# One-hot operands of the PEER gate products, built token by token on VectorE

## The chip, the cores and the metric

The kernel runs on one core of one Trainium2 chip. The metric is the device time of one execution in microseconds. Before the change three runs took 1708.99, 1710.05 and 1712.87 us, median 1710.05 us. The profiled execution, from which all rows below come, took 1712.26 us.

## The reference, cut to what matters

The program is one layer of a diffusion backbone over 512 latent tokens of width 1024 (with 256 context tokens): a mixing part (windowed attention and a gated delta rule), then PEER, a retrieval of single-neuron experts. The change lies in PEER alone:

```
q = (xt @ w_query)                        # 8 heads x 2 halves of 128
s = q . sub_keys                          # 128 keys per half
s_top, i_top = top_k(s, 16)               # per half
best, pos = top_k(all 16 x 16 sums, 16)   # per head
expert = i1 * 128 + i2                    # 128 (head, k) pairs per token, 16384 experts
gate = softmax(best)
act = gelu(u_tab[expert] . xt)
y = sum over the 128 pairs of gate * act * v_tab[expert]
```

Each token thus has 128 triples (i1, i2, gate).

## The kernel before, in words

The 512 tokens lie in four tiles (slots 0 to 3) of 128. For slot 3 the kernel gathers the rows of `peer_u` and `peer_v` that its tokens want (GpSimd indirect DMAs, line 2224, with VectorE sums, lines 2234 and 2256). For slots 0 to 2 (384 tokens) it computes all 16384 experts densely, in 128 blocks e of 128 experts:

- **U product** (`t_usplit`, `t_u`, `t_act`): a block of `peer_u` is loaded, split into two 16-bit parts (ScalarE line 2056, VectorE line 2058, one operation of 1024 elements each), multiplied with the tokens (24 TensorE matmuls of 384 columns through `mm`, line 207) and passed through Gelu (ScalarE line 2091). The split has two slots, so it runs at most two blocks ahead of the matmuls. Results wait in SBUF for the V stage; the number of places for them is limited, and up to 20 more may be written to DRAM.
- **Gates** (`t_gates`, the functions of the diff): a dense 128 x 128 matrix of gates per token, as a product of one-hot matrices. For one token, with its 128 pairs on the partitions, the left operand is onehot(i1), the right one onehot(i2) times the gate; the gate is carried as a high and a low float16 part, so there are two right operands and two 128-column matmuls per token. TensorE transposes i1, i2 and gate of a slot so that the pairs come onto the partitions (line 1952); `pT` holds the transposed columns, one column per token. Then eight chunks of 16 tokens follow per slot, 24 chunks in all. In a chunk VectorE builds three operand blocks `oh[0..2]` of 16 tokens x 128 keys with four whole-chunk operations (lines 1980, 1982, 1984, 1986); TensorE does 32 matmuls into four PSUM banks; ScalarE copies them out (line 1998); a DMA writes the chunk to DRAM (`wd`, line 2003).
- **V product** (`t_wread`, `t_vload`, `t_vsplit`, `t_g`, `t_v`): from the event `ev_wall` on, when all gates have been written, gates are read back, multiplied with the U results (lines 2147, 2152, 2154), `peer_v` is split (lines 2131, 2133), and each block costs 18 matmuls of 512 columns.

The order of each engine's instructions is fixed when the program is built: a planner (`Driver`) simulates the engines with a cost for each step (`dv`, `ac`, `p16`, the table `X`) and hands out the steps by priority (a lower number first; U split 60.5, gates 70 to 72, U matmuls 80.7). On the chip each engine works through its list in that order and waits where a semaphore makes it wait. In `dv(n, p, x)` the planner takes 0.068 us, plus n x 1.042 ns divided by x, plus 0.062 us for each of p scalars per partition.

Of the kernel before, what the change touches and what calls it, by code (L numbers as in the profile page):

```python
# [17 lines left out]
F16 = mybir.dt.float16  # L18
# [3 lines left out]
AF = mybir.ActivationFunctionType  # L22
OP = mybir.AluOpType
# [43 lines left out]
class Driver:  # L67
# [26 lines left out]
    def _advance(self, t, val):  # L94
        while True:
# [20 lines left out]
            else:  # L116
                t.pend = s
                if s[0] == "PE" and t.ready == t.pe:
                    t.ready -= X['lPE']
                self.ready.append(t)  # L120
                return

    def run(self):
        while self.ready or self.blocked:
# [14 lines left out]
            starts = [max(t.ready, self.free[t.pend[0]]) for t in self.ready]  # L139
            m = min(starts) + X['win']  # L140
            i = min((k for k in range(len(starts)) if starts[k] <= m),
# [4 lines left out]
            self.free[e] = end  # L146
            end += X["l" + e]
            if len(t.pend) > 2:
# [7 lines left out]
def get(res, n=1):  # L156
    return ("get", res, n)


def put(res, *items):  # L160
    return ("put", res) + items


def p16(n, m=1):
    return ("PE", m * max(0.027, n / 2400.0 + 0.0025))


def p32(n, m=1):
    return ("PE", m * max(0.107 * X["f32"], n * 0.429 * X["f32"] / 512))


def ptr32(m):
    return ("PE", 0.109 * m)


def dv(n, p=0, x=1):
    return ("DVE", 0.068 + n * 1.042e-3 / x + 0.062 * p)


def ac(n, p=0, sb=0):  # L180
    return ("ACT", 0.051 + 0.042 * sb + n * 0.833e-3 + 0.093 * p)
# [6 lines left out]
def dm(nbytes):  # L188
    return ("DMA", nbytes / 360e3)


def later(step):
    return step + ("a",)


X = {'ch': 6.183, 'gt': 9.96, 'ka': 11.636, 'qa': 6.328, 'z': 10.883, 'ad2': 8.509, 'wo': 14.584, 'a1': 5.91, 'a2': 9.456, 'a0': 10.73, 'a3': 11.524, 'o1': 14.974, 'o2': 11.058, 'o0': 14.074, 'o3': 15.009, 'p00': 4.186, 'p01': 1.683, 'p10': 3.269, 'p11': 4.66, 'p20': 3.974, 'p21': 2.21, 'p30': 5.555, 'p31': 5.48, 'p40': 4.392, 'p41': 9.258, 'p50': 5.369, 'p51': 6.667, 'vg': 0.857, 'ga': 5.978, 'k': 5.749, 'v': 4.787, 'q': 5.8, 'cs': 6.278, 'ro': 10.195, 'vi': 3.54, 'hx': 5.748, 'lPE': 0.1405, 'lDVE': 0.1984, 'lACT': 0.18, 'lPOOL': 0.1344, 'lDMA': 2.0, 'win': 0.1972, 'f32': 2.175, 'pt': 60.784, 'ps': 61.1, 'pg': 70, 'pgc': 70, 'pul': 80.08, 'pus': 60.5, 'pu': 80.677, 'pvs': 75, 'pgg': 74.921, 'pv': 81.055, 'pga': 77, 'pgt': 78, 'pq': 60, 'psc': 60, 'pql': 18, 'pqs': 18, 'pac': 80, 'ptg': 75.5, 'psg': 75.6}


def layer(tc, io, dbg=None):
# [16 lines left out]
def _body(tc, nc, V, A, G, PE, io, dbg, drv, sync, mm, ap_, pp_, dp_):  # L216
# [337 lines left out]
    ev_ada2 = Ev()  # L554
    AD2 = X["ad2"]

# [215 lines left out]
    def evac(dst, b, n, ev, bank):  # L772
        yield ac(n)
        A.activation(dst, b[:, :n], AF.Copy, scale=1.0 / WS)
        yield put(bank, b)
        yield ("set", ev)

    def t_qkv(kind, h, ti):
# [9 lines left out]
        ev_raw = Ev()  # L788
        yield ("spawn", evac(raw[:, 2:514], b, T, ev_raw, bank), X[kind] + 0.1 * h)
        if not lat_only:  # L790
# [848 lines left out]
    for n, t in enumerate((1, 2, 0, 3)):  # L1639
        drv.add(t_out(t), X["o%d" % t])  # L1640

    _peer(nc, V, A, G, PE, io, dbg, drv, sync, mm, reg, bk, bc, Bump, gp4, at3, obk, h2hl, h2d, x1d, modrow, dp_,
          sm, cst, ident, TILE, ev_h2, ev_gdn, ev_attall, ev_odone, stats, bnhalf, moments, fetch)
    drv.run()
# [6 lines left out]
def _peer(nc, V, A, G, PE, io, dbg, drv, sync, mm, reg, bk, bc, Bump, gp4, at3, obk, h2hl, h2d, x1d, modrow, dp_,  # L1651
# [40 lines left out]
    grow = Res([reg(69 + 4 * i, [D]) for i in range(4)])  # L1692
    ust = Res([reg(17 + 4 * i, [KT, 128]) for i in range(3)])
    uhl = Res([(reg(29 + 4 * i, [KT, 128], F16), reg(31 + 4 * i, [KT, 128], F16)) for i in range(2)])
    ohs = Res([[reg(101 + 12 * i + 4 * j, [16, 64, 2], F16) for j in range(3)] for i in range(2)])
    wbs = Res([reg(125 + 8 * i, [128, 16]) for i in range(2)])
    pTs = Res([[reg(141 + 0.5 * (4 * i + j), [128, 2], F16) for j in range(4)] for i in range(2)])
    iota = reg(145, [64, 2], F16)
    vst = Res([reg(101 + 4 * i, [D]) for i in range(3)])
    vhl = Res([(reg(113 + 4 * i, [D], F16), reg(115 + 4 * i, [D], F16)) for i in range(2)])  # L1700
    wrs = Res([reg(121 + 12 * i, [NCH, 8, 16]) for i in range(2)])
# [2 lines left out]
    def actr(kb, n):  # L1704
        return [reg(kb + 1.5 * i, [ND]) for i in range(n)]
# [236 lines left out]
    def t_gates(s):  # L1942
        yield ev_pair[s]
        yield ev_qdone
        yield ev_iota
        k = pairs[s]
        ii = k["ii"]
        b = yield get(wvb)
        ps = bk(b, [3, 128])
        yield ptr32(3)  # L1950
        for n in range(3):
            PE.transpose(ps[:, n], ii[:, n].rearrange("p k h -> p (k h)"), ident)
        yield put(tks, k)
        pT = yield get(pTs)
        def twice(n):
            return bc(ps[:, n, :, None], 128, 2)
        for n in range(2):
            yield later(ac(256))
            A.activation(pT[n], twice(n), AF.Copy)
        yield ac(256)  # L1960
        A.activation(pT[2], twice(2), AF.Copy, scale=1024.0)
        yield dv(256)
        V.scalar_tensor_tensor(pT[3], twice(2), 1024.0, pT[2], op0=OP.mult, op1=OP.subtract)
        yield ("join",)
        yield put(wvb, b)
        left = [8]
        done = Ev()

        def chunk(n):
            tk = slice(n * 16, n * 16 + 16)  # L1970
            oh = yield get(ohs)

            def col(i):
                return bc(pT[i][:, tk, None], 16, 64, 2)
            keys = iota[:, None].to_broadcast([128, 16, 64, 2])

            def row(i, tok):
                return oh[i][:, tok].rearrange("p a b -> p (a b)")
            yield later(dv(2048, 0, 2))
            V.tensor_tensor(oh[0], col(0), keys, op=OP.is_equal)  # L1980
            yield dv(2048, 0, 2)
            V.tensor_tensor(oh[1], col(1), keys, op=OP.is_equal)  # L1982
            yield later(dv(2048, 0, 2))
            V.tensor_tensor(oh[2], oh[1], col(3), op=OP.mult)  # L1984
            yield later(dv(2048, 0, 2))
            V.tensor_tensor(oh[1], oh[1], col(2), op=OP.mult)  # L1986
            yield ("join",)
            wb = yield get(wbs)
            for q in range(4):
                b = yield get(wvb)  # L1990
                ps = bk(b, [4, 128])
                yield p16(128, 8)
                for j in range(4):
                    tok = q * 4 + j
                    mm(ps[:, j], row(0, tok), row(1, tok), j == 0, False)
                    mm(ps[:, j], row(0, tok), row(2, tok), False, j == 3)
                yield later(ac(512))
                A.activation(wb[:, :, q * 4:q * 4 + 4], ps.rearrange("p t i -> p i t"), AF.Copy, scale=GS / 1024.0)  # L1998
                yield put(wvb, b)
            yield put(ohs, oh)  # L2000
            yield ("join",)
            yield dm(128 * 8192)
            sync.dma_start(wd[:, :, s * 8 + n].rearrange("w p i t -> p w i t"), wb.rearrange("p (w i) t -> p w i t", i=8))
            yield put(wbs, wb)
            left[0] -= 1
            if left[0] == 0:
                yield ("set", done)
        for n in range(8):
            yield ("spawn", chunk(n), X["pgc"] + s)
        yield done  # L2010
        yield put(pTs, pT)
        yield ("set", ev_gated[s])
        w_left[0] -= 1
        if w_left[0] == 0:
            yield ("set", ev_wall)
# [4 lines left out]
    def t_iota():  # L2020
        yield ev_qdone
        yield ev_mem1
        yield dm(128 * 256)
        sync.dma_start(iota.rearrange("p a b -> p (a b)"), io["iota"])
        yield put(ohs, [reg(73 + 4 * j, [16, 64, 2], F16) for j in range(3)])
        yield ("set", ev_iota)
        for s in range(3):
            yield ev_pair[s]
        yield put(acts, *acts1)
        for s in range(3):  # L2030
            yield ev_gated[s]
        yield get(tks, 2)
        yield put(acts, *actr(85, 8))
        yield put(tks, tks_late[0])
        yield ev_pair[3]
        yield put(acts, *acts2)
# [284 lines left out]
    for s in range(4):  # L2321
        drv.add(t_slot(s), X['ps'] + 0.2 * s if s != GSLOT else X['psg'])
    drv.add(t_iota(), 60)
    for s in range(3):
        drv.add(t_gates(s), X['pg'] + s)
# [108 lines left out]
```

## Time and profile before

| | before |
|---|---|
| runs | 1708.99, 1710.05, 1712.87 us |
| profiled execution | 1712.26 us, span 1710.5 us |
| TensorE (PE) busy | 1609.8 us, 94% of the span |
| VectorE (DVE) busy | 1444.0 us, 84% |
| ScalarE (ACT) busy | 791.0 us, 46% |
| GpSimd (POOL) busy | 478.1 us, 28% |
| mean granted TensorE clock | 0.984 of full speed |

"Span" is the time from the first to the last recorded instruction of the profiled execution; the execution lasted 1.8 us longer than its span. Busy time is a union: where two instructions of one engine overlap, the overlap counts once. The duration of an instruction is therefore longer than what it costs its engine when another follows at once; that cost is the distance from start to start, and is read from the timeline.

### The profile page before, as it was taken

The page shows a single profiled execution, that of the slowest core. Times are in us where ns is not written, and L with a number is a line of the kernel's source. Part 1 is how long each engine was busy: PE and PEld are TensorE (multiplying, and loading weights), DVE is VectorE, ACT ScalarE, POOL GpSimd, SP SyncE. Part 2 cuts the span into 40 slices and gives each one's busy share as a digit, 9 for nine tenths or more (in the row PEclk, how much of TensorE's full clock was granted, in tenths as well). Part 3 has the DMA queues.
Part 4 walks back from the last instruction along what each step waited for, and adds up shares of the span by engine and source line. Part 5 has one row for each costly group of instructions (what it writes and reads, how often), then busy time and mean ns, then how long its engine had stood idle before and what let it go on. Part 6 is the DMA issues. An engine that isn't in the chain of part 4 may idle for free.

```text
span 1710.5 us, 29276 instructions
## 1 busy us (share of the span) xinstructions
PE 1609.8 (94%) x11075; PEld 978.2 (57%) x11075; DVE 1444.0 (84%) x2884; ACT 791.0 (46%) x1386; POOL 478.1 (28%) x351
## 2 busy tenths in 40 slices
PE   3999998988896999999999999999999999899997
PEld 1665557887655885677655555555555554444443
DVE  3678658988989999999988888888888888798887
ACT  2665658766533434566543333333333333244441
POOL 0200332323001000000014445445466556554300
PEclk9999999999998999999999999999999999999999
DMA  9335442211333303699969999999999999888762
GB/s 378 113 128 187 155 179 81 70 56 45 109 112 134 114 2 124 191 272 279 325 241 354 348 369 344 374 364 350 347 377 330 367 363 331 315 317 331 270 244 86
DMA packets 157727, 405.16 MB, mean 237 GB/s; under 512 B 12681, under 2 KB 71561, under 8 KB 152465
## 3 DMA queue, kind: packets, MB, share of 16 engines
q1 hardware_dynamic: 120720, 269.06, 45.1%
q0 software_dynamic: 36864, 134.23, 21.4%
q8 instruction: 86, 1.41, 0.3%
q14 instruction: 57, 0.46, 0.1%
HBM read 366.59 MB, written 36.65 MB: 236 GB/s over the span
## 4 chain that ended last, share of the span: by engine, by line
PE 39%; DVE 20%; DMA 10%; issue 5%; POOL 2%; ACT 1%; POOLq 0%; DVEq 0%; ACTq 0%; SPq 0%
PE bank L207 38%; DMA arena<-in_peer_v,arena 8%; DVE arena L2058 3%; POOL arena L2224 2%; DVE arena L1986 1%; DVE arena L1984 1%; DVE arena L1980 1%; DVE arena L1982 1%; DVE arena L2256 1%; DMA arena<-in_peer_u,arena 1%; DVE arena L1816 1%; DVE arena L1818 1%; DVE arena L1822 1%; DVE arena L1814 1%; DVE arena L1759 1%
## 5 line engine op out<-in xcount | busy, mean ns | idle before, releaser
L207 PE MATMUL bank<-arena 128*128 128x384 f16 (+9 forms) x10610 | 1566.5, 316 | 49.4 <-DVE arena L1105 6.8
L207 PEld LDWEIGHTS <-arena 128*128 128x128 f16 (+1 forms) x9528 | 826.9, 98 | 626.8 <-issue 46.1
L2224 POOL DMA_INDIRECT arena<-in_peer_u,arena x128 | 161.1, 1258 | 515.2 <-DMA arena<-in_peer_ut 339.0
L2224 POOL DMA_INDIRECT arena<-in_peer_v,arena x128 | 211.8, 1655 | 160.6 <-DVE arena L2256 140.4
L2056 ACT ACTIVATE arena<-arena 128x1024 f16<-128x1024 f32 x128 | 135.1, 1056 | 253.9 <-PE bank L207 184.5
L2131 ACT ACTIVATE arena<-arena 128x1024 f16<-128x1024 f32 x128 | 134.2, 1050 | 136.4 <-PE bank L207 101.0
L2256 DVE SCALAR_TENSOR_TENSOR arena<-arena 128x1024 f32<-128x1024 f32 x126 | 160.2, 1280 | 36.9 <-DMA arena<-in_peer_v,arena 36.7
L2133 DVE TENSOR_TENSOR arena<-arena 128x1024 f16<-128x1024 f32 x128 | 156.0, 1219 | 29.2 <-ACT arena L2131 29.0
L2058 DVE SCALAR_TENSOR_TENSOR arena<-arena 128x1024 f16<-128x1024 f32 x128 | 155.9, 1220 | 26.5 <-ACT arena L2056 26.3
L2234 DVE SCALAR_TENSOR_TENSOR arena<-arena 128x1024 bf16<-128x1024 f32 x128 | 156.3, 1221 | 23.6 <-DMA arena<-in_peer_u,arena 22.8
L2152 ACT ACTIVATE arena<-arena 128x384 f16<-128x384 f32 x128 | 66.4, 519 | 170.6 <-DVE arena L2147 170.4
L207 PEld LDWEIGHTS bank<-arena 128*128 128x128 f32 (+1 forms) x1082 | 114.5, 178 | 36.0 <-DMA arena<-in_w_ada 12.3
L2154 DVE TENSOR_TENSOR arena<-arena 128x384 f16<-128x384 f32 x128 | 70.6, 552 | 6.6 <-ACT arena L2152 6.6
L1063 POOL TENSOR_TENSOR arena<-arena 128x512 f32<-128x512 f32 x12 | 17.9, 1495 | 203.7 <-DVE arena L1060 203.7
L2147 DVE TENSOR_TENSOR arena<-arena 128x384 f32<-128x384 f32 x128 | 70.5, 551 | 1.5 <-DMA arena<-wd 1.5
L1998 ACT ACTIVATE arena<-bank 128x512 f32<-128x512 f32 x96 | 51.7, 598 | 24.9 <-PE bank L207 17.8
L1105 DVE TENSOR_TENSOR arena<-bank,arena 128x512 f16<-128x512 f32 x72 | 49.0, 685 | 15.9 <-PE bank L207 11.5
L2091 ACT ACTIVATE arena<-bank 128x384 f32<-128x384 f32 x128 | 60.7, 475 | 1.6 <-DVE arena L2154 1.2
L1113 ACT ACTIVATE arena<-bank 128x512 f16<-128x512 f32 x60 | 35.8, 597 | 22.4 <-PE bank L207 21.3
L810 DVE SCALAR_TENSOR_TENSOR arena<-arena 128x770 f32<-128x770 f32 (+1 forms) x48 | 44.1, 928 | 0.8
L1529 POOL TENSOR_TENSOR arena<-arena 128x1024 f32<-128x1024 f32 x4 | 9.4, 2348 | 116.5 <-DVE arena L1527 104.0
L1118 ACT ACTIVATE arena<-bank 128x512 f16<-128x512 f32 x60 | 35.5, 596 | 6.2 <-PE bank L207 4.5
(256 smaller groups left out, 1275.0 us busy)
## 6 DMA issues: line engine op xcount, KB each, us to landing
arena<-in_peer_ut SPq DMA_DIRECT2D x128, 512.0 KB, 5.8
arena<-in_peer_v SPq DMA_DIRECT2D x128, 512.0 KB, 6.4
arena<-in_w_ada SPq DMA_DIRECT2D x24, 1024.0 KB, 8.7
wd<-arena SPq DMA_DIRECT2D x24, 1024.0 KB, 6.9
arena<-wd SPq DMA_DIRECT2D x16, 1536.0 KB, 10.3
arena<-in_w_int SPq DMA_DIRECT2D x21, 512.0 KB, 4.4
arena<-in_wq SPq DMA_DIRECT2D x16, 512.0 KB, 3.6
arena<-in_x SPq DMA_DIRECT2D x8, 512.0 KB, 4.6
```

The lines of the kernel that those rows point to most:

```text
L207: PE.matmul(out, lhsT=l, rhs=r, start=start, stop=stop, skip_group_check=True)
L2056: A.activation(hl[0], Ud[e], AF.Copy, scale=US)
L2058: V.scalar_tensor_tensor(hl[1], Ud[e], US, hl[0], op0=OP.mult, op1=OP.subtract)
L2091: A.activation(Aw[e], b[:, 0:ND], AF.Gelu, scale=1.0 / US)
L2131: A.activation(hl[0], Vd[e], AF.Copy)
L2133: V.tensor_tensor(hl[1], Vd[e], hl[0], op=OP.subtract)
L2147: V.tensor_tensor(a3, a3, Wr[w][:, :, e % 8], op=OP.mult)
L2152: A.activation(g[0], a, AF.Copy)
L2154: V.tensor_tensor(g[1], a, g[0], op=OP.subtract)
L2224: G.indirect_dma_start(out=r, out_offset=None, in_=io[name], in_offset=bass.IndirectOffsetOnAxis(ap=gidx[:, p:p + 1], axis=0))
L2234: V.scalar_tensor_tensor(scr, r, 1.0, h2g, op0=OP.mult, op1=OP.mult, accum_out=gact[:, p:p + 1])
L2256: V.scalar_tensor_tensor(y, r, gact[:, p:p + 1], y, op0=OP.mult, op1=OP.add)
```

## The change

The four whole-chunk operations on broadcast columns become 48 operations per chunk, three per token, each over 128 keys. A key row `iota` (128 float16 values) is compared with a scalar per partition (the token's column of `pT`, float32 now); for the two right operands a second scalar, the gate part, is multiplied in within the same instruction. The planner is told 0.095 us for each. The columns are no longer stored twice, and the low gate part is now made from the float32 value and a float16 copy of it (`g16`), which adds one ScalarE operation per slot.

```diff
-X = {'ch': 6.183, ...
+X = {'oh': 0.095, 'ch': 6.183, ...
...
-    ohs = Res([[reg(101 + 12 * i + 4 * j, [16, 64, 2], F16) for j in range(3)] for i in range(2)])
+    ohs = Res([[reg(101 + 12 * i + 4 * j, [16, 128], F16) for j in range(3)] for i in range(2)])
-    pTs = Res([[reg(141 + 0.5 * (4 * i + j), [128, 2], F16) for j in range(4)] for i in range(2)])
-    iota = reg(145, [64, 2], F16)
+    pTs = Res([[reg(141 + 0.5 * (4 * i + j), [128]) for j in range(4)] for i in range(2)])
+    pT16s = Res([reg(145.25 + 0.25 * i, [128], F16) for i in range(2)])
+    iota = reg(145, [128], F16)
...
-        def twice(n):
-            return bc(ps[:, n, :, None], 128, 2)
+        g16 = yield get(pT16s)
         for n in range(2):
-            yield later(ac(256))
-            A.activation(pT[n], twice(n), AF.Copy)
-        yield ac(256)
-        A.activation(pT[2], twice(2), AF.Copy, scale=1024.0)
-        yield dv(256)
-        V.scalar_tensor_tensor(pT[3], twice(2), 1024.0, pT[2], op0=OP.mult, op1=OP.subtract)
+            yield later(ac(128))
+            A.activation(pT[n], ps[:, n], AF.Copy)
+        yield ac(128)
+        A.activation(pT[2], ps[:, 2], AF.Copy, scale=1024.0)
+        yield ac(128, 0, 1)
+        A.activation(g16, pT[2], AF.Copy)
+        yield dv(128)
+        V.tensor_tensor(pT[3], pT[2], g16, op=OP.subtract)
...
-            def col(i):
-                return bc(pT[i][:, tk, None], 16, 64, 2)
-            keys = iota[:, None].to_broadcast([128, 16, 64, 2])
-
             def row(i, tok):
-                return oh[i][:, tok].rearrange("p a b -> p (a b)")
-            yield later(dv(2048, 0, 2))
-            V.tensor_tensor(oh[0], col(0), keys, op=OP.is_equal)
-            yield dv(2048, 0, 2)
-            V.tensor_tensor(oh[1], col(1), keys, op=OP.is_equal)
-            yield later(dv(2048, 0, 2))
-            V.tensor_tensor(oh[2], oh[1], col(3), op=OP.mult)
-            yield later(dv(2048, 0, 2))
-            V.tensor_tensor(oh[1], oh[1], col(2), op=OP.mult)
+                return oh[i][:, tok]
+
+            def at(i, tok):
+                return pT[i][:, n * 16 + tok:n * 16 + tok + 1]
+            for tok in range(16):
+                yield later(("DVE", X["oh"]))
+                V.tensor_scalar(row(0, tok), iota, at(0, tok), None, op0=OP.is_equal)
+                for i in (1, 2):
+                    yield later(("DVE", X["oh"]))
+                    V.tensor_scalar(row(i, tok), iota, at(1, tok), at(i + 1, tok), op0=OP.is_equal, op1=OP.mult)
             yield ("join",)
```

## Rows read from the trace of the kernel before

**Rows 1.** The page's first part: busy time, share of the span, instructions of two engines.

```profile
PE 1609.8 (94%) x11075; PEld 978.2 (57%) x11075; DVE 1444.0 (84%) x2884; ACT 791.0 (46%) x1386; POOL 478.1 (28%) x351
```

**Rows 2.** Busy time by stage: stretch, its length, busy us (instructions), clock, DMA share, GB/s.

```profile
640.00:680.00 40.00, 39.15 (x240) 23.06 (x239) 40.00 (x195) 19.39 (x30) 0.00 (x0) 1.00 0.37 119
680.00:836.00 156.00, 152.81 (x1439) 108.33 (x1438) 155.70 (x177) 94.46 (x158) 0.00 (x0) 1.00 0.86 252
836.00:861.00 25.00, 21.23 (x128) 12.14 (x127) 23.40 (x134) 10.13 (x16) 0.00 (x0) 1.00 0.97 345
861.00:1690.00 829.00, 819.94 (x4276) 419.04 (x4276) 700.10 (x926) 317.22 (x429) 372.89 (x256) 0.99 0.89 327
```

**Rows 3.** The chain that ended last, 733 to 861 us: start, us, what.

```profile
733.17 1.13 DVE arena L1980
734.30 1.14 DVE arena L1984
...
831.70 1.14 DVE arena L1986
...
836.61 7.05 DMA wd<-arena
...
843.74 7.07 DMA arena<-wd
```

**Rows 4.** Groups by line and form, 680 to 836 us: busy us, mean ns, idle before.

```profile
L2058 DVE SCALAR_TENSOR_TENSOR arena<-arena 128x1024 f16<-128x1024 f32 x28 | 34.1, 1218 | 0.2 <-ACT arena L2056 0.2
L1986 DVE TENSOR_TENSOR arena<-arena 128x2048 f16<-128x2048 f16 x24 | 29.1, 1218 | 0.1
L207 PE MATMUL bank<-arena 128*128 128x384 f16 x668 | 116.1, 326 | 0.3 <-DVE arena L2058 0.3
L207 PE MATMUL bank<-arena 128*128 128x128 f16 x768 | 50.2, 219 | 2.9 <-DVE arena L1986 2.8
```

**Rows 5.** DVE's timeline around one whole-chunk operation: start, duration in us.

```profile
703.59 1.22 DVE L1986 TENSOR_TENSOR arena<-arena 128x2048 f16<-128x2048 f16 x1
704.73 1.22 DVE L1910 TENSOR_TENSOR arena<-arena 128x2048 f16<-128x2048 f16 x1
705.86 1.22 DVE L1986 TENSOR_TENSOR arena<-arena 128x2048 f16<-128x2048 f16 x1
707.00 1.22 DVE L2058 SCALAR_TENSOR_TENSOR arena<-arena 128x1024 f16<-128x1024 f32 x1
```

**Rows 6.** DVE's timeline: operations of 128 elements with constants, then of 1 element.

```profile
619.85 0.76 DVE L1872 TENSOR_SCALAR arena<-arena 128x128 uint32<-128x128 uint32 x5
620.53 0.22 DVE L1874 CAST arena<-arena 128x128 f32<-128x128 uint32 x1
...
1693.42 0.15 DVE L384 TENSOR_SCALAR arena<-arena 128x1 uint32<-128x1 uint32 x1
1693.49 0.14 DVE L386 TENSOR_SCALAR arena<-arena 128x1 f32<-128x1 f32 x1
```

**Rows 7.** DVE's timeline: operations with scalars per partition (L490 two, others one).

```profile
18.68 2.25 DVE L490 TENSOR_SCALAR arena<-arena 128x1024 f32<-128x1024 f32 x3
20.85 1.35 DVE L635 SCALAR_TENSOR_TENSOR arena<-arena 128x1152 f16<-128x1152 f32 x1
...
265.85 0.33 DVE L1356 TENSOR_SCALAR arena<-arena 128x1 f32<-128x1 f32 x2
...
1239.58 0.75 DVE L2254 TENSOR_SCALAR arena<-arena 128x1024 f32<-128x1024 f32 x1
1240.24 1.22 DVE L2058 SCALAR_TENSOR_TENSOR arena<-arena 128x1024 f16<-128x1024 f32 x1
```

**Rows 8.** All instructions of one line: count, ns min/median/max, first and last start, form.

```profile
L490 DVE TENSOR_SCALAR arena<-arena x3: 808/808/809, 18.7 to 20.1; 128x1024 f32<-128x1024 f32 x3
L1356 DVE TENSOR_SCALAR arena<-arena x32: 161/206/215, 265.8 to 483.0; 128x1 f32<-128x1 f32 x32
L1959 ACT ACTIVATE arena<-bank x6: 366/376/384, 639.8 to 752.4; 128x256 f16<-128x256 f32 x6
L1963 DVE SCALAR_TENSOR_TENSOR arena<-bank,arena x3: 401/412/414, 678.0 to 755.9; 128x256 f16<-128x256 f32 x3
```

**Rows 9.** An earlier stretch in which PE had long gaps: columns as in rows 2.

```profile
520.00:540.00 20.00, 13.83 (x97) 11.66 (x98) 18.62 (x38) 8.96 (x15) 4.69 (x2) 0.74 0.42 137
```

More of the change, by code (lines that the diff above doesn't have):

```diff
@@ L193, in later @@
     return step + ("a",)
-X = {'ch': 6.183, 'gt': 9.96, 'ka': 11.636, 'qa': 6.328, 'z': 10.883, 'ad2': 8.509, 'wo': 14.584, 'a1': 5.91, 'a2': 9.456, 'a0': 10.73, 'a3': 11.524, 'o1': 14.974, 'o2': 11.058, 'o0': 14.074, 'o3': 15.009, 'p00': 4.186, 'p01': 1.683, 'p10': 3.269, 'p11': 4.66, 'p20': 3.974, 'p21': 2.21, 'p30': 5.555, 'p31': 5.48, 'p40': 4.392, 'p41': 9.258, 'p50': 5.369, 'p51': 6.667, 'vg': 0.857, 'ga': 5.978, 'k': 5.749, 'v': 4.787, 'q': 5.8, 'cs': 6.278, 'ro': 10.195, 'vi': 3.54, 'hx': 5.748, 'lPE': 0.1405, 'lDVE': 0.1984, 'lACT': 0.18, 'lPOOL': 0.1344, 'lDMA': 2.0, 'win': 0.1972, 'f32': 2.175, 'pt': 60.784, 'ps': 61.1, 'pg': 70, 'pgc': 70, 'pul': 80.08, 'pus': 60.5, 'pu': 80.677, 'pvs': 75, 'pgg': 74.921, 'pv': 81.055, 'pga': 77, 'pgt': 78, 'pq': 60, 'psc': 60, 'pql': 18, 'pqs': 18, 'pac': 80, 'ptg': 75.5, 'psg': 75.6}
+X = {'oh': 0.095, 'ch': 6.183, 'gt': 9.96, 'ka': 11.636, 'qa': 6.328, 'z': 10.883, 'ad2': 8.509, 'wo': 14.584, 'a1': 5.91, 'a2': 9.456, 'a0': 10.73, 'a3': 11.524, 'o1': 14.974, 'o2': 11.058, 'o0': 14.074, 'o3': 15.009, 'p00': 4.186, 'p01': 1.683, 'p10': 3.269, 'p11': 4.66, 'p20': 3.974, 'p21': 2.21, 'p30': 5.555, 'p31': 5.48, 'p40': 4.392, 'p41': 9.258, 'p50': 5.369, 'p51': 6.667, 'vg': 0.857, 'ga': 5.978, 'k': 5.749, 'v': 4.787, 'q': 5.8, 'cs': 6.278, 'ro': 10.195, 'vi': 3.54, 'hx': 5.748, 'lPE': 0.1405, 'lDVE': 0.1984, 'lACT': 0.18, 'lPOOL': 0.1344, 'lDMA': 2.0, 'win': 0.1972, 'f32': 2.175, 'pt': 60.784, 'ps': 61.1, 'pg': 70, 'pgc': 70, 'pul': 80.08, 'pus': 60.5, 'pu': 80.677, 'pvs': 75, 'pgg': 74.921, 'pv': 81.055, 'pga': 77, 'pgt': 78, 'pq': 60, 'psc': 60, 'pql': 18, 'pqs': 18, 'pac': 80, 'ptg': 75.5, 'psg': 75.6}
 def layer(tc, io, dbg=None):
@@ L1954, in t_gates @@
         pT = yield get(pTs)
-        def twice(n):
-            return bc(ps[:, n, :, None], 128, 2)
+        g16 = yield get(pT16s)
         for n in range(2):
-            yield later(ac(256))
-            A.activation(pT[n], twice(n), AF.Copy)
-        yield ac(256)
-        A.activation(pT[2], twice(2), AF.Copy, scale=1024.0)
-        yield dv(256)
-        V.scalar_tensor_tensor(pT[3], twice(2), 1024.0, pT[2], op0=OP.mult, op1=OP.subtract)
+            yield later(ac(128))
[6 more added lines that the diff above has]
+        V.tensor_tensor(pT[3], pT[2], g16, op=OP.subtract)
         yield ("join",)
         yield put(wvb, b)
+        yield put(pT16s, g16)
         left = [8]
@@ L2023, in t_iota @@
         yield dm(128 * 256)
-        sync.dma_start(iota.rearrange("p a b -> p (a b)"), io["iota"])
-        yield put(ohs, [reg(73 + 4 * j, [16, 64, 2], F16) for j in range(3)])
+        sync.dma_start(iota, io["iota"])
+        yield put(ohs, [reg(73 + 4 * j, [16, 128], F16) for j in range(3)])
         yield ("set", ev_iota)
```

## The prediction, as recorded before the result

> **What bounds the kernel now.** I read the page's busy times first, then the busy time by stage, then the chain of waits, and last the timeline of VectorE. The busy times make TensorE the bound of the whole, 94% against VectorE's 84% [rows 1]; but that is a mean over stages, and the change lies in one stage, that of the gates (680 to 836 us). There both are full: PE is busy 152.81 of 156 us and DVE 155.70 [rows 2]. Which of them sets the pace is told by the chain: from 733 to 832 us it runs through the whole-chunk operations and the U splits on DVE, hands over to the write and the read-back of the gates, and only after 861 us to PE [rows 3]. DVE's idle time ahead of these operations is 0.1 us in all; PE's ahead of the gate matmuls is 2.9 us, ended by the last operation of a chunk [rows 4]. So in this stage every microsecond that DVE gains or loses moves the end of the stage, with PE only about 3 us behind as the next limit. After 861 us PE is busy 819.94 of 829 us and DVE 700.10 [rows 2]: a delay that reaches that point isn't made up there.
>
> **The change part by part.**
>
> *Removed.* 24 chunks of four operations, 96 in all. One lasts 1.218 us [rows 4] but costs less, since the next starts before its end: from start to start it is 1.14, 1.13 and 1.14 us [rows 5], on average 1.135. 96 x 1.135 = 109.0 us.
>
> *Added.* 16 x 3 x 24 = 1152 operations of 128 elements: 384 with one scalar per partition and 768 with two. Their cost from start to start has three parts.
> The fixed part: five operations of 128 elements with constants take 0.68 us from the first start to the next operation's, 0.136 each [rows 6]; a one-element operation takes 0.07 [rows 6]. The difference, 0.066 us, is 128 elements at two per cycle (0.52 ns each), so the fixed part is 0.07.
> The scalars: an operation of 1024 elements with one scalar takes 0.66 us to the next start, of which 0.533 are elements, which leaves 0.127; two of one element with one scalar span 0.33 us at 0.206 each, 0.124 from start to start [rows 7, 8]. Three of 1024 elements with two scalars take 2.17 us to the next start, 0.723 each, less 0.533 leaves 0.190 [rows 7]. So fixed part and scalars are 0.125 us with one scalar, 0.190 with two, for long and short operations alike; the load of a scalar isn't hidden behind the operation ahead, not even a short one.
> The elements: no row shows a one-source operation from 16-bit to 16-bit. Two things are seen apart. 2048 16-bit elements of two sources cost 1.135 us, as do 1024 of 32 bits [rows 5]: 16-bit data halve the time. 1024 32-bit elements of one source cost 0.533 us beside the fixed part [rows 7], half of what two sources take: one source halves it too. Either alone gives 0.067 us for 128 elements, both together 0.033. I take both together, as the two halvings come from different properties, and keep 0.067 as the other end.
> The Trainium skill lists this case ("VectorE: DVE Perf Modes", the perf-mode tier table): a tensor_scalar on 16-bit data in SBUF runs at four elements per cycle, a tensor_tensor at two. By it the elements cost 0.033 us, my value; no run here shows such an operation yet.
> One token thus costs 0.158 + 2 x 0.223 = 0.604 us, and 384 tokens 231.9 us, where 109.0 were. DVE gets 122.9 us more work. At two elements per cycle it is 0.703 per token, 270.0 us, +161. If the elements run wholly under the fixed part and the scalars, it is 0.125 + 2 x 0.190 = 0.505, 193.9 us, +85. If nothing overlapped (0.750 us - 0.533 = 0.217 with one scalar, 0.808 - 0.533 = 0.275 with two [rows 7, 8], each plus 0.033), it is 0.866, 332.5 us, +223.
>
> *What lies beside it.* DVE has no idle time in the stage, so all of it is on the path. PE cannot fill the gap: its list was fixed by a planner that takes 0.095 us for an operation, 48 x 0.095 = 4.56 us for a chunk where it took 4.54 before, so about the same 28 U blocks [rows 4] are put between the same chunks, and PE waits. The stage becomes about 279 us long with 153 us of work for PE. PE's granted clock may fall in the gaps; in a stretch with 13.83 of 20 us of PE work it was 0.74 [rows 9]. At 0.74 the 153 us become 207, still less than 279, so I put nothing on it, and 5 us as a bound for the return to full clock.
> ScalarE, SyncE's queue and the gate writes keep their number and order, only later. The gathers of slot 3 start behind the gates and shift with them.
>
> *The columns.* Per slot ScalarE does four copies of 128 elements in place of three of 256 (0.376 us each, line 1959 [rows 8]), VectorE one of 128 in place of one of 256 from PSUM (0.412, line 1963 [rows 8]). The new copy stands ahead of VectorE's, which adds one hop between the engines; behind it wait the chunk's operations. From -0.4 to +0.5 us per slot, three slots: taken as 0.
>
> *At the end of the stage* the matmuls of a token can start when its three rows are there and not when a whole chunk is, which may give back 1 to 2 us once: inside the rounding.
>
> *Sum.* 1712.3 us for the profiled execution (span 1710.5 and 1.8 around it) + 122.9 = 1835. The median of the runs is 2.2 us under the profiled one, so the median after should be 1832 to 1833; I say 1832.
>
> **The rivals.**
> *Scalars per partition are free in a train of short operations.* Then one costs 0.07 + 0.033 = 0.103 us, 1152 cost 118.7, +10, 1722; at the planner's 0.095 it is 109.4 us and nothing changes, 1710. For it: no row has many short two-scalar operations in a row. Against it: the pair of one-element operations, 0.124 from start to start where 0.07 is seen without a scalar [rows 6, 7].
> The Trainium skill has a rule that leads there ("VectorE: DVE Perf Modes", the section on the TRN2 errata): an operation from SBUF to SBUF costs 58 cycles plus its elements over the mode's factor. At 0.96 GHz that is an estimate of 94 ns for 128 elements at four per cycle, 108 us for all, no change. The trace agrees for constants (127 ns by the rule, 136 measured [rows 6]) but shows some 60 ns on top for each scalar, which the rule doesn't count. The same section advises operations of at least 512 elements, so that the fixed cost is spread; these have 128.
>
> *The other side: faster.* If short operations overlap down to the 0.07 us of a one-element operation, 1152 cost 80.6 us, DVE is relieved by 28 us and PE is the bound. The point from which it decides is a mean cost of 109.0 / 1152 = 0.0946 us. The gain then ends at PE's idle time, 3.2 us in the stage and 3.8 up to 861 us [rows 2]: 1703 to 1707. Against it: it needs free scalars and free elements.
>
> *Only two elements per cycle.* +161: 1871. For it: no row shows four.
>
> *PE gets ahead.* If the finer steps let the planner put more U blocks into the stage, each moves PE work of 24 x 384 columns (152.81 us for 668 x 384 + 768 x 128 columns [rows 2, 4], so 4.0 us) into the gap for 1.135 us of DVE: 2.8 us back per block. Ten blocks give 1804. The same range is reached if elements are partly hidden (+85: 1795).
>
> **How the numbers follow.** The forecast, 1820 to 1850: 0.61. Two per cycle, 1860 to 1885: 0.12. Partly hidden or more U blocks, 1785 to 1820: 0.08. Scalars free, 1706 to 1725: 0.09. Faster with PE as the bound: 0.06. Worse than 1885, operations that don't overlap, up to 1933: 0.04. The range 1785 to 1885 holds 0.81; the forecast's own range is 1820 to 1850. By 0.2% (3.4 us, about what a measurement of this kernel can tell from no change): of the 0.09, 0.01 is faster, 0.05 within and 0.03 slower. So faster 0.07, same 0.05, slower 0.88.
>
> **What would show it.** In the profile after: the one-scalar line 0.16 us from start to start, the two-scalar lines 0.22; DVE still without idle time in a stage of about 280 us; PE busy for a little over half of it, its waits ended by the new lines; after the stage the same 830 us of PE work. Wrong would be: starts 0.1 us apart (scalars free), 0.19 and 0.26 (two per cycle), many more than 28 U splits in the stage, or DVE idle there.

## The result, and the profile after

The changed kernel takes 1851.74 us (median of 4 runs, 1847.60 to 1854.39) against 1711.22 us before in the same comparison: ratio 1.0818, 95% interval 1.0798 to 1.0838. It is 140.5 us slower; 122.9 were forecast. The time lies in the stated range (1785 to 1885) and 2 us outside the forecast's own (1820 to 1850).

The page's busy times after, which answer to [rows 1]. PE's busy time grew by 48 us, DVE's by 125:

```profile
PE 1657.3 (89%) x11075; PEld 1000.7 (54%) x11075; DVE 1569.4 (85%) x3940; ACT 792.7 (43%) x1389; POOL 469.5 (25%) x351
```

Busy time by stage after, columns as in [rows 2]: the stage before the gates, the gates, the hand-over to the V stage, the V stage.

```profile
640.00:683.00 43.00, 42.15 (x260) 25.00 (x258) 43.00 (x215) 21.44 (x34) 0.00 (x0) 1.00 0.36 111
683.00:970.00 287.00, 210.06 (x1513) 135.15 (x1512) 287.00 (x1259) 101.49 (x167) 0.00 (x0) 0.85 0.49 144
970.00:1000.00 30.00, 4.99 (x26) 2.47 (x24) 25.46 (x127) 6.41 (x9) 0.00 (x0) 0.61 0.88 289
1000.00:1830.00 830.00, 821.55 (x4291) 420.14 (x4289) 688.92 (x899) 314.85 (x427) 364.25 (x256) 1.00 0.89 326
```

The V stage is what it was (830 us here, 829 in [rows 2]). The loss lies ahead of it, and two things stand out. The gate stage grew from 156 to 287 us, with DVE busy in every microsecond of it. And in the hand-over PE does 26 matmuls in 30 us, where it did 128 in 25 before [rows 2].

The timeline of DVE in the changed kernel, start and duration in us, answers to [rows 5]. L1983 is the comparison with one scalar, L1986 the one with two.

```profile
724.21 1.41 DVE L1986 TENSOR_SCALAR arena<-arena 128x128 f16<-128x128 f16 x6
725.55 0.56 DVE L1983 TENSOR_SCALAR arena<-arena 128x128 f16<-128x128 f16 x3
726.04 1.41 DVE L1986 TENSOR_SCALAR arena<-arena 128x128 f16<-128x128 f16 x6
```

Six operations with two scalars take 725.55 - 724.21 = 1.34 us, 0.223 each; three with one scalar 0.49 us, 0.163 each. The working had 0.223 and 0.158. So 1152 operations cost 768 x 0.223 + 384 x 0.163 = 233.9 us (231.9 forecast), 124.9 more than the 109.0 removed. Who waits is shown by PE's groups in the stage after (busy us, mean ns, then idle time before and its releasers), against 0.3 and 2.9 us in [rows 4]:

```profile
L207 PE MATMUL bank<-arena 128*128 128x384 f16 x755 | 152.6, 360 | 45.0 <-DVE arena L2058 44.4 <-ACT arena L2091 0.7
L207 PE MATMUL bank<-arena 128*128 128x128 f16 x768 | 72.3, 246 | 31.5 <-DVE arena L1986 31.2
```

PE's idle time stands in front of the U matmuls (the U split waits its turn between the small operations) and in front of the gate matmuls. That leaves 140.5 - 124.9 = 15.6 us. PE's timeline at the hand-over shows where to look. Before:

```profile
835.81 12.84 PE L207 MATMUL bank<-arena 128*128 128x384 f16 x78
848.81 3.91 PE L207 MATMUL bank<-arena 128*128 128x384 f16 x23 [0.17 <-DVE arena L2058]
853.32 0.32 PE L207 MATMUL bank<-arena 128*128 128x384 f16 x1 [0.60 <-ACT arena L2091]
854.68 4.34 PE L207 MATMUL bank<-arena 128*128 128x384 f16 x25 [1.04 <-DVE arena L2058]
861.00 1.52 PE L207 MATMUL bank<-arena 128*128 128x512 f16 x4 [1.97 <-DVE arena L2133]
```

and after (the first row begins with the last gate matmuls):

```profile
965.47 7.96 PE L207 MATMUL bank<-arena 128*128 128x128 f16 x57 [0.18 <-DVE arena L1986]
998.19 1.01 PE L207 MATMUL bank<-arena 128*128 128x512 f16 x2 [24.77 <-ACT arena L2131]
```

The gates' write and read-back lie on the chain in both kernels (7.05 and 7.07 us before [rows 3], 10.83 and 8.31 after). Before, PE worked through U blocks meanwhile; after, it sits idle for 24.77 us. The U matmuls that PE does between the last gate matmul and the first V matmul are called the bridge below.

### The profile page after: what moved, and what is told of

Same layout as the page of the kernel before. It is cut to its first block, busy times and chain, and to the rows that moved or that the text cites. A ratio compares the mean times of both kernels' runs of the same rounds, so it can differ in the third digit from the quotient of the medians.

```text
span 1852.2 us, 30352 instructions
## 1 busy us (share of the span) xinstructions
PE 1657.3 (89%) x11075; PEld 1000.7 (54%) x11075; DVE 1569.4 (85%) x3940; ACT 792.7 (43%) x1389; POOL 469.5 (25%) x351
## 4 chain that ended last, share of the span: by engine, by line
PE 36%; DVE 27%; DMA 8%; issue 5%; POOL 3%; ACT 1%; POOLq 0%; DVEq 0%; SPq 0%; ACTq 0%
PE bank L207 35%; DVE arena L1986 9%; DMA arena<-in_peer_v,arena 6%; DVE arena L1983 3%; DVE arena L2058 3%; POOL arena L2224 3%; DVE arena L2256 1%; DVE arena L1819 1%; DVE arena L1817 1%; DMA wd<-arena 1%; DVE arena L1823 1%; DVE arena L1815 0%; DVE arena L1760 0%; DMA arena<-wd 0%; PE bank L1381 0%
## 5 line engine op out<-in xcount | busy, mean ns | idle before, releaser
L207 PE MATMUL bank<-arena 128*128 128x384 f16 (+9 forms) x10610 | 1613.0, 320 | 142.6 <-DVE arena L2058 44.9
L207 PEld LDWEIGHTS <-arena 128*128 128x128 f16 (+1 forms) x9528 | 847.6, 100 | 746.5 <-issue 89.6
L2056 ACT ACTIVATE arena<-arena 128x1024 f16<-128x1024 f32 x128 | 135.2, 1056 | 304.1 <-PE bank L207 226.7
L2224 POOL DMA_INDIRECT arena<-in_peer_v,arena x128 | 204.0, 1594 | 164.4 <-DVE arena L2256 139.2
L1986 DVE TENSOR_SCALAR arena<-arena 128x128 f16<-128x128 f16 x768 | 192.0, 297 | 0.0
L1998 ACT ACTIVATE arena<-bank 128x512 f32<-128x512 f32 x96 | 54.0, 597 | 109.0 <-PE bank L207 82.6
L1983 DVE TENSOR_SCALAR arena<-arena 128x128 f16<-128x128 f16 x384 | 82.0, 236 | 0.0
L1113 ACT ACTIVATE arena<-bank 128x512 f16<-128x512 f32 x60 | 35.8, 597 | 23.2 <-PE bank L207 21.7
```

Of the source, the lines that this page charges most:

```text
L207: PE.matmul(out, lhsT=l, rhs=r, start=start, stop=stop, skip_group_check=True)
L1983: V.tensor_scalar(row(0, tok), iota, at(0, tok), None, op0=OP.is_equal)
L1986: V.tensor_scalar(row(i, tok), iota, at(1, tok), at(i + 1, tok), op0=OP.is_equal, op1=OP.mult)
L2056: A.activation(hl[0], Ud[e], AF.Copy, scale=US)
L2224: G.indirect_dma_start(out=r, out_offset=None, in_=io[name], in_offset=bass.IndirectOffsetOnAxis(ap=gidx[:, p:p + 1], axis=0))
```

## The experiments

Times are medians; a difference in us with a plus sign is against the kernel before, run beside the variant on the same chip (1711.31 us for the first four variants, 1711.94 us for the late places and for told cost and hold together, 1712.8 us for the others). A difference from the changed kernel is one of medians, against 1851.74 us.

**Constants in place of scalars.**

```diff
-V.tensor_scalar(row(0, tok), iota, at(0, tok), None, op0=OP.is_equal)
+V.tensor_scalar(row(0, tok), iota, 5.0, None, op0=OP.is_equal)
...
-    V.tensor_scalar(row(i, tok), iota, at(1, tok), at(i + 1, tok), op0=OP.is_equal, op1=OP.mult)
+    V.tensor_scalar(row(i, tok), iota, 7.0, 8.0, op0=OP.is_equal, op1=OP.mult)
```

> The changed kernel with constants in place of the scalars per partition: every token compares with the keys 5 and 7 and multiplies by 8, so the gates are not those of the reference. All 1152 operations, their order and TensorE's per-token waits stay. Theory A (the price is VectorE's, and mostly the loading of scalars): an operation costs 0.07 + 0.033 = 0.103 us from start to start, 118.7 us in all instead of 233.5, and the time falls to 1722 us, 1712 to 1737. Rival B (the price is the grain: 1152 instructions and a wait of TensorE per token, and its clock): the time stays over 1800 us.

Measured 1738.16 us, ratio 1.0139 (1.0093 to 1.0185), +26.9. DVE's timeline of this kernel, three and six operations in a row:

```profile
716.51 0.39 DVE L1983 TENSOR_SCALAR arena<-arena 128x128 f16<-128x128 f16 x3
716.82 0.69 DVE L1986 TENSOR_SCALAR arena<-arena 128x128 f16<-128x128 f16 x6
717.43 0.28 DVE L1965 TENSOR_TENSOR arena<-arena 128x128 f32<-128x128 f32 x1
```

0.61 us for six, 0.102 each. With the number of operations, their order and the fine waits unchanged, taking the scalars away takes 114 of the 141 us. B falls. The time is 1 us above A's range, which is less than the four runs differ among themselves (1732.90 to 1743.36 us). But operations that cost 118 us, 9 more than those they replace, leave 18 us unexplained (the interval allows 7 to 23), about as many as in the changed kernel. The clock and the waits inside the stage don't explain them, for here PE is busy in nearly all of it, at full clock (columns as in [rows 2]):

```profile
683.00:850.00 167.00, 162.34 (x1469) 112.92 (x1467) 166.78 (x1227) 93.54 (x159) 0.00 (x0) 1.00 0.82 240
```

**One scalar in each operation.**

```diff
-    V.tensor_scalar(row(i, tok), iota, at(1, tok), at(i + 1, tok), op0=OP.is_equal, op1=OP.mult)
+    V.tensor_scalar(row(i, tok), iota, at(1, tok), 8.0, op0=OP.is_equal, op1=OP.mult)
```

> The changed kernel with one scalar per partition in each operation: the key comes from the scalar, the gate is the constant 8, so the gates' values are not those of the reference. Theory A: 0.158 us each, 182 us in all, 51 less than in the changed kernel; with the surplus in proportion 1785 to 1800 us. Rival B: no change from 1852 us. If only the second scalar of an instruction costs something, it is as fast as the run with constants.

Measured 1806.49 us, 1.0542 (1.0501 to 1.0583), +95.2: above the 1785 to 1800 that A had. The timeline of this kernel:

```profile
715.87 1.06 DVE L1986 TENSOR_SCALAR arena<-arena 128x128 f16<-128x128 f16 x6
716.85 0.57 DVE L1983 TENSOR_SCALAR arena<-arena 128x128 f16<-128x128 f16 x3
```

0.98 us for six, 0.163 each: 0.061 more than with constants, and 0.060 less than with two scalars. What A had wrong was the surplus: it isn't in proportion to the price of the operations.

**Keys in float32.** A copy of the key row in float32 (`iota32`, made once) takes the place of `iota` in the three operations.

> The changed kernel with the key row in float32 instead of float16; same results. If 128 float16 keys run at four per cycle (theory A), the float32 row makes it two: 0.033 us more for each of 1152 operations, +38 us, 1890 us (1880 to 1900), and the two lines stand 0.195 and 0.257 us from start to start. If the keys were at two per cycle already, nothing changes, 1852 us.

Measured 1892.38 us, 1.1039 (1.0994 to 1.1083), +181.1, as A expected. In its timeline the same operations stand at 1.54 / 6 = 0.257 and 0.59 / 3 = 0.197 us:

```profile
720.01 1.63 DVE L1987 TENSOR_SCALAR arena<-arena 128x128 f16<-128x128 f32 x6
721.55 0.68 DVE L1984 TENSOR_SCALAR arena<-arena 128x128 f16<-128x128 f32 x3
722.14 0.35 DVE L1987 TENSOR_SCALAR arena<-arena 128x128 f16<-128x128 f32 x1
```

That is 0.034 us more each for reading 32-bit keys. It is what follows if 128 float32 keys take 0.067 us and 128 float16 keys half of that, 0.033.

These three and the changed kernel lie on one line, with a surplus that doesn't depend on the price. All four have the same order of U work, since the planner is told the same 0.095 us in each:

| kernel | us per operation (left, right) | 1152 operations | more than 109.0 | measured | surplus |
|---|---|---|---|---|---|
| constants | 0.102, 0.102 | 118 | 9 | 26.9 | 18 |
| one scalar | 0.163, 0.163 | 188 | 79 | 95.2 | 16 |
| changed kernel | 0.163, 0.223 | 234 | 125 | 140.5 | 16 |
| float32 keys | 0.197, 0.257 | 273 | 164 | 181.1 | 17 |

**The planner told the measured cost** (`'oh': 0.203` in place of 0.095).

> The changed kernel with the planner told 0.203 us for an operation, the mean of the two measured costs, in place of 0.095; same instructions in another order. Theory A: VectorE's 233.5 us stay, and the planner can only put more U blocks into the gaps of TensorE, each worth 4.0 us of TensorE for 1.135 us of VectorE, as far as there are places for their results; 10 blocks more give 28 us back: 1815 to 1845 us. Rival C (the loss is a wrong order, made from a wrong cost): most of the 141 us come back, under 1770 us. If places for results run out at once, no change, 1852.

Measured 1830.98 us, 1.0687 (1.0647 to 1.0728): 21 us better than the changed kernel, in A's range. C falls. The order has the splits of 57 U blocks ahead of the first V matmul instead of 45; 20 results went out to DRAM instead of 8, which is all that the program allows. This order has no U matmul left for the hand-over, and PE's idle time there is 24.18 us as before.

**Slot 3 held back.** The surplus was sought in the order of the work. Between the last gate matmul and the first V matmul stand 126 U matmuls before the change, 24 after and 24 with constants. In the changed kernel slot 3's selection takes one of the two top-k buffers during the gate stage; eight places for U results lie in such a buffer and are handed out when both are free, so there they come only behind slot 3.

```diff
         yield ev_top[s]
+        if s == GSLOT:
+            yield ev_wall
         k = yield get(tks)
```

> The changed kernel with slot 3's top-k selection (t_slot) held back until all gates are written; same results, same operations. Theory D: some 17 us of the 141 have nothing to do with the operations' price. They come from the order: in the changed kernel slot 3 takes one of the two top-k buffers during the gate stage, so the eight places for U results that lie in it come free only behind slot 3, and PE has 24 instead of 126 U matmuls to bridge the write and read-back of the gates (PE is idle for some 24 us there). With the hold there are 144. D expects 1830 to 1840 us and PE's idle time ahead of the first V matmul down from 25 to a few us. Rival: the 17 us are lost inside the gate stage (TensorE's clock, finer waits); then 1847 to 1857 us.

Measured 1834.36 us, 1.0717 (1.0695 to 1.0740): 17 us better than the changed kernel, as D expected. The stage itself is unchanged (287 us, PE clock 0.85); the hand-over of this kernel, answering to the third row of the table by stage above, has 124 matmuls in place of 26:

```profile
683.00:970.00 287.00, 208.90 (x1514) 134.67 (x1513) 287.00 (x1258) 101.09 (x167) 0.00 (x0) 0.85 0.50 144
970.00:1000.00 30.00, 22.20 (x124) 12.39 (x123) 22.30 (x119) 8.87 (x14) 0.00 (x0) 0.89 0.93 326
```

**The same loss put into the kernel before.** The eight places are handed out behind slot 3's selection, with the whole-chunk operations of before.

```diff
-        yield put(acts, *actr(85, 8))
         yield put(tks, tks_late[0])
         yield ev_pair[3]
+        yield put(acts, *actr(85, 8))
```

> The kernel before with the eight places for U results handed out only behind slot 3's selection, as it came out in the changed kernel; same results, the gate operations of before. PE then has 30 instead of 126 U matmuls to bridge the write and read-back of the gates. Theory D: 96 x 0.16 = 15 us slower, 1724 to 1732 us, with some 15 to 24 us of PE idle ahead of the first V matmul. Rival (the missing bridge costs nothing, the rest of the changed kernel's loss lies in its stage): 1708 to 1716 us.

Measured 1729.18 us, 1.0094 (1.0063 to 1.0124): 17 us slower than the kernel before, as D expected, without a single operation of the change. Its PE timeline at the hand-over:

```profile
834.67 7.80 PE L207 MATMUL bank<-arena 128*128 128x128 f16 x68 [0.43 <-DVE arena L1986]
861.05 1.01 PE L207 MATMUL bank<-arena 128*128 128x512 f16 x2 [18.59 <-ACT arena L2131]
```

So a missing bridge costs about 17 us, shown from both sides. It does not follow that the changed kernel lost its surplus in just this way. The U matmuls ahead of the first V matmul, in groups (columns as in [rows 4]), are 1056 before, 1032 in the changed kernel, 1152 with the hold and 960 here:

```profile
L207 PE MATMUL bank<-arena 128*128 128x384 f16 x1056 | 180.5, 326 | 2.4 <-DVE arena L2058 1.7 <-ACT arena L2091 0.6
L207 PE MATMUL bank<-arena 128*128 128x384 f16 x1032 | 198.5, 351 | 45.4 <-DVE arena L2058 44.6 <-ACT arena L2091 0.7
L207 PE MATMUL bank<-arena 128*128 128x384 f16 x1152 | 219.2, 349 | 53.7 <-DVE arena L2060 47.6 <-ACT arena L2093 6.1
L207 PE MATMUL bank<-arena 128*128 128x384 f16 x960 | 164.4, 326 | 0.6 <-DVE arena L2058 0.5
```

The hold thus puts 120 U matmuls into time in which PE was idle, and this kernel leaves 96 more for the V stage: at 0.165 us each (78 in 12.84 us at the hand-over before) 20 and 16 us. The changed kernel leaves only 24 more than the kernel before, since most of what its bridge lacks is done earlier. Its surplus is spread, and the traces of before and after let it be followed. The profiled execution became 141.7 us longer. VectorE's last gate operation ends 135.9 us later: 124.4 for the price of the operations, 6.7 for parts of slot 3's first top-k (the 16 best of each half; the other slots need theirs before their gates), 3.4 for the splits of three more U blocks, 1.4 for idle time. From there to the first V matmul it takes 3.9 us more, and behind it 2.0. All instructions of one line of that top-k, before and after (columns as in [rows 8]), show how its last start moved from 836.6 us, behind the gate operations, to 737.4, among them:

```profile
L1816 DVE FIND_INDEX8 arena<-arena x64: 276/285/300, 538.7 to 836.6; 128x8 uint32<-128x128 f32 x64
L1817 DVE FIND_INDEX8 arena<-arena x64: 273/280/293, 540.8 to 737.4; 128x8 uint32<-128x128 f32 x64
```

The kernel with the hold has the same 6.7 and 3.4 us in its stage. So the hold makes up for the surplus with U work; it does not take its parts away. Why the planner moved them was not followed up.

**One part undone: the left operand by whole chunks.** The columns of i1 are stored twice again for it (`pT0`).

```diff
+        pT0 = pT[0].bitcast(F16).rearrange("p (a b) -> p a b", b=2)
...
+            yield later(dv(2048, 0, 2))
+            V.tensor_tensor(oh[0].rearrange("p t (a b) -> p t a b", b=2), bc(pT0[:, n * 16:n * 16 + 16, None], 16, 64, 2),
+                            iota.rearrange("p (a b) -> p a b", b=2)[:, None].to_broadcast([128, 16, 64, 2]), op=OP.is_equal)
             for tok in range(16):
-                yield later(("DVE", X["oh"]))
-                V.tensor_scalar(row(0, tok), iota, at(0, tok), None, op0=OP.is_equal)
```

> One part of the change undone: the left operand (oh[0]) is again made by one whole-chunk operation, the two right operands stay token by token; same results. Theory A, price by price: 16 x 0.162 = 2.6 us per chunk go, 1.135 come, 24 chunks: -35 us, 1817 us (1808 to 1826). If a first operation with one scalar cost nothing because the others hide it, no gain: 1850 or more.

Measured 1824.85 us, 1.0656 (1.0638 to 1.0673). That is 27 us better than the changed kernel instead of 35, inside the range. The price came out as expected: up to the last gate operation, VectorE's operand operations cost 35.2 us less in its trace than in the changed kernel's. What is missing lies in the order: 18 matmuls are left as a bridge, and 936 U matmuls stand ahead of V instead of 1032, so that 96 more, 16 us of PE, wait behind; VectorE's other work ahead of that point shrinks by some 7 us.

**How much VectorE could have gained.** The kernel before without line 1984, slot 3 held back.

```diff
-            yield later(dv(2048, 0, 2))
-            V.tensor_tensor(oh[2], oh[1], col(3), op=OP.mult)
...
-                    mm(ps[:, j], row(0, tok), row(2, tok), False, j == 3)
+                    mm(ps[:, j], row(0, tok), row(1, tok), False, j == 3)
```

> The kernel before without the operation of line 1984 (the low gate part is left out and the high part multiplied twice), with slot 3 held back as in the other run. VectorE is relieved by 24 x 1.135 = 27 us in the gate stage. If PE is the next limit as the prediction has it (3.2 us idle in the stage, 3.8 behind it), at most 7 us come back: 1704 to 1711 us. If VectorE alone sets the stage, 27 us: 1684.

Measured 1713.45 us, 1.0001 (0.9989 to 1.0013): 27 us less work for VectorE and no gain at all, the lower end of the 0 to 7 us that were expected. In this kernel DVE is busy 143.97 of the 156 us and PE still 148.41:

```profile
680.00:836.00 156.00, 148.41 (x1407) 105.26 (x1405) 143.97 (x277) 92.15 (x157) 0.00 (x0) 1.00 0.92 273
```

With VectorE relieved, PE's 1029.5 us of busy time between 640 and 1690 us remain (1033.1 before [rows 2]), and the end doesn't move. The gates are ready 28 us earlier, but the shorter stage has room for fewer U matmuls: 912 stand ahead of V instead of 1056, and the 144 others, 24 us of PE, wait behind. A faster way to build the operands had nothing to win in this order; another order was not tried.

**A part moved to GpSimd.** The kernel before, with slot 3 held back and the low operand of every second chunk made there:

```diff
+            if n % 2:
+                yield pl(2048)
+                G.tensor_tensor(oh[2], oh[1], col(3), op=OP.mult)
+            else:
+                yield later(dv(2048, 0, 2))
+                V.tensor_tensor(oh[2], oh[1], col(3), op=OP.mult)
```

> The kernel before with the low right operand (line 1984) of every second chunk on GpSimd, idle in this stage, and slot 3 held back; same results. VectorE is relieved by 12 x 1.135 = 14 us; one GpSimd operation should take about 6 us (1.495 us for 512 elements on its line 1063, times four), 72 us of 150. If PE is the next limit and GpSimd does not disturb VectorE: 1703 to 1711 us. If the two engines disturb each other or the operand comes late, slower than before: 1715 to 1740 us.

Measured 1748.41 us, 1.0211 (1.0197 to 1.0225): slower, the rival's side and worse than it said. The twelve GpSimd operations (POOL) take 3.61 to 12.49 us. GpSimd's timeline and VectorE's in this kernel:

```profile
773.28 3.61 POOL L1987 TENSOR_TENSOR arena<-arena 128x2048 f16<-128x2048 f16 x1 [10.69 <-DVE arena L1984]
787.39 3.61 POOL L1987 TENSOR_TENSOR arena<-arena 128x2048 f16<-128x2048 f16 x1 [10.50 <-DVE arena L1984]
```

```profile
773.40 4.57 DVE L1982 TENSOR_TENSOR arena<-arena 128x2048 f16<-128x2048 f16 x1
777.90 1.21 DVE L1984 TENSOR_TENSOR arena<-arena 128x2048 f16<-128x2048 f16 x1
787.80 4.28 DVE L1982 TENSOR_TENSOR arena<-arena 128x2048 f16<-128x2048 f16 x1 [0.55 <-PE bank L207]
```

Both times VectorE's operation ends 1.08 us after GpSimd's (777.97 after 776.89, 792.08 after 791.00), whenever it started. The trace has ten such, of 3.27 to 4.63 us in place of 1.21: they cost VectorE 28 us where 14 were taken off it. And the high operand overwrites what GpSimd reads, so it comes after it, and PE waits for that line (28.3 us in 12 waits). How the 36 us divide between the two isn't shown.

**Told cost and hold together.** Both edits above in one kernel.

> The changed kernel with both: the planner told 0.203 us for an operation, and slot 3 held back; same results. PE has 62 U blocks ahead of the first V matmul (57 with the cost alone, 50 with the hold alone, 45 in the changed kernel) and 120 matmuls as a bridge. If the two effects add (-21 and -17 us) 1810 to 1820 us. If they are one effect (a place for U work, whatever its source), 1825 to 1835 us. VectorE's 124 us stay in either case.

Measured 1824.12 us, 1.0660 (1.0625 to 1.0695): 28 us better than the changed kernel, neither the 38 of two separate effects nor the 21 of one. The order has 120 matmuls as a bridge, and in the trace the splits of 61 blocks ahead of V (48 with the hold alone). That both edits make room for U work and overlap in part fits these counts, but which block is worth what stays open. No variant of the token-by-token form that makes the right gates came near the kernel before, and no run beat it.

## Why the prediction was right, and where it was not

- **The bound** was read rightly. DVE set the gate stage, its extra work became length of the stage in full, and nothing came back in the V stage (829 and 830 us). PE as the next limit close behind holds too: with 27 us less for DVE it gave nothing, within the 7 us of the prediction.
- **The price of an operation** was right in all three parts, from rows of quite other operations [rows 6 to 8]. The fixed part with the keys was forecast as 0.103 us and measured as 0.102; a scalar 0.055 to 0.065 and 0.060 to 0.061; the keys at four per cycle 0.033, and 0.034 more for 32 bits. The sum was 122.9 and came out as 124.9. (Two figures of the working are slightly off, without effect: at two elements per cycle its parts give 0.706 us per token, not 0.703, and 10 us on the median of 1710 is 1720, not 1722.)
- **The rival "scalars free"** fell on the measured 0.061 us per scalar; with it the rule of fixed cycles plus elements that the prediction took from the Trainium skill ("VectorE: DVE Perf Modes", the section on the TRN2 errata). By the rule the operation costs an estimated 94 ns; the run with constants shows 102, the changed kernel 163 and 223. The same section of the Trainium skill advises against operations under 512 elements. The trace agrees: per token, operations of 128 elements cost 0.61 us where those of 2048 cost 0.284. The four elements per cycle of the Trainium skill ("VectorE: DVE Perf Modes", the perf-mode tier table) agree with the float32 run, 0.034 us more for 128 keys of 32 bits.
- **The rival "faster"** had the right size of what could be won (at most 3 to 7 us) and a condition, 0.0946 us per operation, that even constants don't meet.
- **The step that failed** is the order of the work, put at nothing. "At the end of the stage" was put down as a gain of 1 to 2 us, with "ScalarE, SyncE's queue and the gate writes keep their number and order, only later". Between the first and the last gate matmul the U work did stay the same, as "about the same 28 U blocks" has it (522 U matmuls before, 528 after). But around it the order changed: the bridge over the gates' way through DRAM shrinks from 126 to 24 U matmuls, 72 more stand ahead of the first gate matmul, and parts of slot 3's first top-k move into the stage, where VectorE has no time to spare. In the four kernels with the order of the changed one this came to 16 to 18 us, of which the traces of before and after show 11.5 up to the end of the gate operations, 3.9 at the hand-over and 2.0 behind it. It took the time from the forecast's 1832 to 1852. That such a loss can be bought back by a bridge is shown by the hold (17 us).
- **The granted clock** fell to 0.85 in the stage, as was allowed for. It isn't the surplus: with constants the clock was 1.00 from 683 to 850 us, and the surplus was 18 us all the same.

## What to carry to other kernels

Before one long operation is replaced by many short ones, take the cost from start to start, fixed part, scalars and elements apart, from whatever rows have them, and compare per unit of work: here 0.284 us per token (4 x 1.135 / 16) against 0.61. Where two engines are both full, a saving on one is worth at most the other's idle time (nothing here for 27 us), while a loss counts in full. And where an order is planned ahead, a change of one stage also moves work of others: count in the built order what stands between the last producer and the first consumer, and what other work has come into the stage that sets the pace.

## What the runs showed of the hardware beyond what was expected

A 2048-element float16 multiply on GpSimd and a long two-source operation on VectorE did not run side by side. In the ten cases of the trace in which such a VectorE operation started beside the GpSimd one, it ended 1.08 us after it (in place of 1.21 us it took 3.27 to 4.63), while GpSimd's own time went from 3.61 up to 12.49 us where VectorE was already in a run of long operations. Small VectorE operations (MAX8 of 128 elements, 0.27 us) kept their time beside it.
